# A diffusion backbone step: the held-over f tiles go, the last token slice is taken in pairs, and five pieces of code move

## The chip, the cores and the metric

One core of a Trainium2 chip runs the whole program in one launch. The metric is device time in microseconds (us). The core has TensorE (PE) for matrix products, VectorE (DVE), ScalarE (ACT), GpSimd (POOL) and SyncE (SP), which issues the DMAs. TensorE writes its sums into eight banks of 128 x 512 numbers in PSUM; DVE and ACT read them there.

## The reference

Two layers work on 640 tokens (128 context, 512 latent) of width 1024. Each layer is half an FFN, a mixer, and half an FFN; every sub-layer is wrapped in two norms with modulation.

```python
def _half_ffn(x, m, k, g_pre, g_post, w1, w2):
    h = _modulated_prenorm(x, g_pre, m, k)        # rmsnorm(x) * (1 + scale) + shift
    return x + 0.5 * m[:, 3 * k + 2, None] * _rmsnorm(_swiglu(h, w1, w2), g_post)

def _swiglu(h, w1, w2):
    gate, up = jnp.split(h @ w1, 2, axis=-1)      # 1024 -> 2 x 2816
    return (jax.nn.silu(gate) * up) @ w2          # 2816 -> 1024

for i in range(DEPTH):                            # DEPTH = 2
    xp, xs = half_ffn(xp), half_ffn(xs)           # context, latent
    # layer 0: 2-D DFT over positions and group channels between two 1024 x 1024 projections
    # layer 1: 16 heads; context attends to context, latent to an 8 x 16 neighbourhood and a cached context
    xp = xp + m_ctx[:, 5, None] * _rmsnorm(yp, norm_post[i, 1])
    xs = xs + m_lat[:, 5, None] * _rmsnorm(ys, norm_post[i, 1])
    xp, xs = half_ffn(xp), half_ffn(xs)
```

All is float32. The outputs are both token groups and the new keys and values.

## The kernel before, in words

The six sub-layers are numbered n = 0 to 5: FFN, Fourier, FFN, FFN, attention, FFN. A float32 product is made of three products of reduced type: each operand is split into `hi` (ACT, line 231) and `lo` = operand − hi (DVE, line 232), and `mm3` (lines 244 to 246) issues hi·hi, lo·hi and hi·lo. Weights come as units of 128 x 1024 (512 KB): a DMA to a `raw` tile, then the split into tiles `hi` and `lo`, of which there are six each. `unit(i)` asks for units up to three ahead of the one that is used. Activations live in a ring of 20 blocks (`ring`), split as well.

The PSUM banks have names: four `main`, two `score`, one `turn`, one `sum`.

FFN: 22 f tiles (128 of the 2816 hidden columns each). f tiles 0 to 3 are done plainly (`w1`): `multi` takes four units at a time and goes over them in turn, for half 0 (320 tokens) and then half 1. From f tile 4 on, `w1_fast` computes both halves with sums of weights and of tokens, seven blocks instead of eight, from four pieces of weights. After each slice of f tiles (`SLICES`, the last is 16 to 22), `w2` multiplies the slice's hidden rows with w2 for each of five token tiles of 128 tokens: per unit six matmuls of 512 columns into two banks; the partial sums are kept in `y` and ACT seeds the banks with them before the next slice. f tiles 20 and 21 (`LATE`) are held over: their last two products stand behind tiles 0 and 1 of the last slice (`tail`), with a weight unit made by `mix`.

When a token tile is complete, `chain` runs: ACT squares both halves (L580), the root is made (L566 on DVE, then POOL's power, L567), DVE multiplies with root and gate (L583), adds to x (L590, in the last sub-layer L628 with a DMA out), ACT sums squares (L599), DVE adds (L564), POOL takes the power again, DVE scales (L602). After a wait, counted in the planner's own estimate of TensorE's time (`yield 9000`, `tick`, `launch`), TensorE transposes the tile in eight pieces (L607) into `turn` and `sum`, ACT and DVE scale and shift them (L616, L618), and the results are split. `finish(half)` makes sure that tiles 0 to 2 (half 0) or 3 and 4 (half 1) are done before their half is used by the next sub-layer.

`gates(n)` transposes the gate columns (L548), sends them through DRAM and loads them back to all partitions as `total` (latent) and `square` (context). `gemv` (L439) is a product of the modulation on DVE with 512 KB of weights; these jobs are put in the background by `behind`.

Fourier: eight units of the input projection, half by half, `fold` on DVE (L929 to L934) after each group of four in half 1, then the two transforms and the output projection. Attention: head placements (`put`, L1057, L1076), scores (L1238), softmax (maximum by L1241, exp on ACT, L1224), context scores (L1248 to L1253), then transposes (L1274) and the output projection. The order in which instructions are put into each engine's queue comes from the order of the code, from `high_priority`, `issue_after` and `behind_of`, and from the planner's estimate; TensorE then executes its queue in that order.

## Time and profile before

| what | value |
|---|---|
| runs | 2256.93, 2260.87, 2263.44 us, median 2260.87 |
| profiled execution | 2258.16 us; its span, first to last instruction, 2256.4 us |
| busy | PE 98%, DVE 75%, ACT 52%, POOL 2% |
| mean TensorE clock | 0.996 |
| DMA | 284.20 MB, mean 126 GB/s |
| FFN 0 to Fourier | seam at about 462 us |
| Fourier to FFN 2 | seam at about 620 us |
| FFN 2 to FFN 3 | seam at about 1050 us |
| FFN 3 to attention | seam at about 1490 us |
| attention to FFN 5 | seam at about 1815 us |

Lines of the trace name an engine, a line of the kernel, the operation and its tiles as out <- in. A name in brackets is what ended the engine's idle time before the instruction.

### The profile page before, as it was taken

How to read it: one execution, taken by the hardware profiler on the slowest of the kernel's cores; microseconds unless marked ns; L12 is line 12 of the kernel's file. 1: busy time of each engine (PE TensorE's matmuls, PEld its weight loads, DVE VectorE, ACT ScalarE, POOL GpSimd, SP SyncE). 2: the span in 40 equal slices, each digit the busy share in tenths (PEclk: the TensorE clock that was granted, in tenths of full speed). 3: DMA queues.
4: the chain of work that ended last, by engine and by line, in shares of the span. 5: the costliest groups of instructions: out<-in, count | busy, mean ns of one | idle time of the engine just before them, and what ended most of it. 6: DMA issues, size and time to landing. Idle time of an engine off the chain costs nothing.

```text
span 2256.4 us, 35213 instructions
## 1 busy us (share of the span) xinstructions
PE 2210.1 (98%) x13730; PEld 2050.1 (91%) x13730; DVE 1686.8 (75%) x3079; ACT 1163.5 (52%) x2200; POOL 51.7 (2%) x95
## 2 busy tenths in 40 slices
PE   7999999999999999999999999999999999999998
PEld 5999999899799999988999999889999799999996
DVE  5898898667768898877688888675676566766674
ACT  4445454454444455446445555475778644455543
POOL 0000000000000000001000000010000000000000
PEclk9999999999999999999999999999999999999999
DMA  8144444423423344434144353523332222322223
GB/s 314 64 150 157 133 148 140 172 94 103 155 95 127 129 146 135 159 120 180 66 140 143 119 157 128 182 77 112 95 121 85 98 89 94 113 89 89 94 94 131
DMA packets 83463, 284.20 MB, mean 126 GB/s; under 512 B 9344, under 2 KB 14304, under 8 KB 83168
## 3 DMA queue, kind: packets, MB, share of 16 engines
q1 hardware_dynamic: 82752, 281.30, 37.0%
q8 instruction: 107, 1.75, 0.3%
q10 hardware_dynamic: 544, 0.66, 0.1%
q14 instruction: 60, 0.49, 0.1%
HBM read 270.34 MB, written 11.58 MB: 125 GB/s over the span
## 4 chain that ended last, share of the span: by engine, by line
PE 67%; DVE 14%; DMA 10%; ACT 5%; issue 3%; POOL 1%; SPq 0%; DVEq 0%; POOLq 0%; ACTq 0%
PE main L244 11%; PE main L246 11%; PE main L245 11%; PE score L246 5%; PE score L245 5%; PE score L244 5%; DVE lo L232 4%; DMA raw<-in_w_mod_t 3%; DMA raw<-in_w 3%; DVE junk L439 3%; PE turn L244 3%; PE turn L245 3%; PE turn L246 3%; PE sum L246 3%; PE sum L245 3%
## 5 line engine op out<-in xcount | busy, mean ns | idle before, releaser
L231 ACT ACTIVATE hi<-raw 128x1024 fp32r<-128x1024 f32 (+1 forms) x366 | 351.3, 971 | 321.0 <-PE score L245 86.1
L232 DVE TENSOR_TENSOR lo<-raw,hi 128x1024 fp32r<-128x1024 f32 (+1 forms) x366 | 406.0, 1115 | 138.8 <-ACT hi L231 137.5
L244 PE MATMUL main<-hi,ring 128*128 128x512 f32 (+2 forms) x1136 | 428.1, 379 | 2.5 <-ACT hi L231 2.5
L245 PE MATMUL main<-lo,ring 128*128 128x512 f32 (+2 forms) x1136 | 426.8, 376 | 0.9 <-DVE lo L232 0.8
L246 PE MATMUL main<-hi,ring 128*128 128x512 f32 (+1 forms) x1136 | 425.1, 375 | 1.4 <-DVE ring L232 1.4
L439 DVE SCALAR_TENSOR_TENSOR junk<-raw,wide 128x1024 bf16<-128x1024 f32 x256 | 313.2, 1224 | 102.3 <-DMA raw<-in_w_mod_t 97.6
L244 PE MATMUL score<-ring,hi 128*128 128x320 f32 x1040 | 321.8, 309 | 0.3 <-ACT left L667 0.3
L246 PE MATMUL score<-ring,lo 128*128 128x320 f32 x1040 | 321.9, 310 | 0.2 <-DVE lo L232 0.2
L245 PE MATMUL score<-ring,hi 128*128 128x320 f32 x1040 | 321.3, 309 | 0.0
L244 PEld LDWEIGHTS main<-hi,ring 128*128 128x128 f32 x1136 | 213.4, 188 | 43.1 <-ACT hi L231 4.8
L245 PEld LDWEIGHTS main<-lo,ring 128*128 128x128 f32 x1136 | 214.0, 188 | 39.7 <-DVE lo L232 3.2
L246 PEld LDWEIGHTS main<-hi,ring 128*128 128x128 f32 x1136 | 213.7, 188 | 39.3 <-DVE ring L232 1.6
L795 ACT ACTIVATE y<-main 128x512 f32<-128x512 f32 x160 | 94.2, 591 | 200.4 <-PE main L246 199.5
L244 PEld LDWEIGHTS score<-ring,hi 128*128 128x128 f32 x1040 | 195.2, 188 | 1.2 <-ACT left L667 0.6
L246 PEld LDWEIGHTS score<-ring,lo 128*128 128x128 f32 x1040 | 195.2, 188 | 1.1 <-DVE lo L232 0.6
L245 PEld LDWEIGHTS score<-ring,hi 128*128 128x128 f32 x1040 | 195.2, 188 | 0.6
L244 PE MATMUL main<-ring,hi 128*128 128x320 f32 x560 | 180.8, 323 | 1.6 <-ACT ring L231 1.6
L244 PE MATMUL turn<-ring,hi 128*128 128x320 f32 x576 | 178.9, 311 | 1.0 <-DVE left L729 0.6
L245 PE MATMUL turn<-ring,hi 128*128 128x320 f32 x576 | 178.0, 309 | 0.0
L246 PE MATMUL turn<-ring,lo 128*128 128x320 f32 x576 | 178.0, 309 | 0.0
L246 PE MATMUL main<-ring,lo 128*128 128x320 f32 x560 | 174.6, 312 | 1.8 <-DVE lo L232 1.8
L245 PE MATMUL main<-ring,hi 128*128 128x320 f32 x560 | 174.3, 311 | 1.0 <-DVE ring L232 1.0
(240 smaller groups left out, 4194.9 us busy)
## 6 DMA issues: line engine op xcount, KB each, us to landing
raw<-in_w SPq DMA_DIRECT2D x264, 512.0 KB, 3.9
raw<-in_w_mod_t SPq DMA_DIRECT2D x128, 512.0 KB, 3.5
raw<-in_qkv SPq DMA_DIRECT2D x26, 512.0 KB, 3.6
first<-in_w_mod_k SPq DMA_DIRECT2D x16, 512.0 KB, 8.7
spill<-ring SPq DMA_DIRECT2D x12, 640.0 KB, 2.9
ring<-spill SPq DMA_DIRECT2D x12, 640.0 KB, 8.5
raw<-in_bias SPq DMA_DIRECT2D x16, 448.0 KB, 3.6
raw<-in_four_in SPq DMA_DIRECT2D x8, 512.0 KB, 6.8
```

What stands on the lines that cost most here:

```text
L231: a = self.nc.scalar.activation(hi, src, AF.Copy)
L232: return a, self.nc.vector.tensor_tensor(lo, src, hi.bitcast(F32), op=ALU.subtract)
L244: mm(out, whi, xhi, start=start, stop=False)
L245: mm(out, whi, xlo, start=False, stop=False)
L246: self.latest = mm(out, wlo, xhi, start=False, stop=stop)
L439: last = self.nc.vector.scalar_tensor_tensor(out=self.junk, in0=raw, scalar=1.0, in1=self.wide[:, cond, :], op0=ALU.mult, op1=ALU.mult, ac ...
L795: nc.scalar.activation(place(i, a), bank_of(i, a), AF.Copy)
```

## The change

- The held-over f tiles go. f tiles 20 and 21 run as all others.
- In the last slice `w2` takes token tiles (0, 1), (2,), (3, 4): each unit is used for both tiles of a pair (in sub-layer 5, 3 and 4 apart). Tile 0, and tile 4 where it is in a pair, use the two `score` banks, which start empty; the sums kept in `y` are added by DVE at the head of the chain (`acc`). `out_proj` takes its tiles in the same pairs.
- `gates(n)` stands two f tiles ahead.
- In `chain`, the gate is multiplied apart from the root, and the root is multiplied and x added in one operation per piece of x. The waits before the transposes are set by tile; tiles 3 and 4 are transposed into `score` banks. The next sub-layer's first `multi` uses `turn` and `sum` instead of `score`.
- Fourier: the background jobs are spread over four places.
- Attention: one value unit is split before the placements, which stand behind its split. The context scores use one operation that adds a zero column block, stores the negated scores in SBUF and takes the minimum.

```diff
@@ chain
-    def chain(self, n, i, pss):
+    def chain(self, n, i, pss, acc=()):
...
+            for ps, a in zip(pss, acc):
+                tt(ps, ps, a, op=ALU.add)
             ss = self.col(3)
             for a, ps in enumerate(pss):
                 copy(place[:, a * WIDE : (a + 1) * WIDE], ps, AF.Square, scale=D ** -0.5, accum_out=ss[:, a : a + 1])
+            tt(pss[0], pss[0], gate[0], op=ALU.mult)
             r = self.root(ss[:, :1], ss[:, 1:2])
-            for ps, g in zip(pss, gate):
-                nc.vector.scalar_tensor_tensor(out=ps, in0=ps, scalar=r, in1=g, op0=ALU.mult, op1=ALU.mult)
+            with self.behind_of(self.rooted):
+                tt(pss[1], pss[1], gate[1], op=ALU.mult)
+            x = self.xpieces(n + 1, i)
+            for t, lo, hi in x:
+                nc.vector.scalar_tensor_tensor(out=t, in0=pss[lo // WIDE][:, lo % WIDE : lo % WIDE + hi - lo], scalar=r,
+                                               in1=t, op0=ALU.mult, op1=ALU.add)
                 if last:
-                    self.leave(n, i, pss, ps)
+                    nc.sync.dma_start(out=self.io["x_out"][i * P : (i + 1) * P, lo:hi], in_=t)
...
-            x = self.xpieces(n + 1, i)
-            for t, lo, hi in x:
-                tt(t, t, pss[lo // WIDE][:, lo % WIDE : lo % WIDE + hi - lo], op=ALU.add)
...
-        yield 9000
-        turned = [self.bank(kind) for kind in ("turn", "sum")]
+        yield {0: 10500, 1: 14000, 2: 9200, 3: 11000, 4: 15000}[i]
+        turned = [self.bank(kind) for kind in (("score", "score") if i > 2 else ("turn", "sum"))]
@@ ffn: the first multi, w2, the plan
-                                 ("main", "main", "score", "score"))
+                                 ("main", "main", "turn", "sum"))
...
+            pss = {i: seed(s, i, (s, i) in fresh) for i in tiles}
...
                 w = self.unit(base + self.w2_at[s] + f - f0)
-                x = [g[f][:, part, i * P : (i + 1) * P] for part in range(2)]
...
+                for i in tiles:
+                    x = [g[f][:, part, i * P : (i + 1) * P] for part in range(2)]
+                    new = s == 0 or (s, i) in fresh
+                    for a in range(2) if a0 is None else (a0,):
+                        cols = slice(a * WIDE, (a + 1) * WIDE)
+                        self.mm3(pss[i][a], *x, w[0][:, cols], w[1][:, cols], new and f == f0, f == f1 - 1, not new)
...
+        fresh = {(end, 0)} if final else {(end, 0), (end, 4)}
...
         for f in FAST:
+            if f == NF - 2:
+                plan += [("gates", None, None)]
             plan += [("fast", f, None)]
...
-        plan += [("mix", f, None) for f in LATE]
         plan += [("x", None, None)]
-        plan += [("w2", (due, i), None) for i in (0, 1)]
-        plan += [("tail", f, None) for f in LATE]
-        plan += [("w2", (due, i), None) for i in range(2, TILES)]
+        plan += [("w2", (due, tiles), None) for tiles in ((0, 1), (2,), (3, 4))]
@@ out_proj
-        for tiles, kind in (((0, 1), "main"), ((2,), "score"), ((3,), "main"), ((4,), "main")):
+        for tiles, kinds in (((0, 1), ("main", "main")), ((2,), ("score",)), ((3, 4), ("main", "score"))):
@@ fourier
-                kinds = ("main", "main", "main" if half or m0 else "score", "main" if half or m0 else "score")
+                kinds = ("main",) * 4 if half or m0 else ("main", "main", "turn", "sum")
...
-                    self.behind(3)
+                self.behind((2, 3, 0, 1)[2 * half + m0 // 4])
@@ attention
-        put = products([("q", 0), ("k", 0), ("q", 1), ("k", 1)], 0, ("main", "main", "score", "score"))
+        put = products([("q", 0), ("k", 0), ("q", 1), ("k", 1)], 0, ("main", "main", "turn", "sum"))
         self.finish(1)
-        with self.behind_of(*self.ready):
+        self.unit(early["v1", 0], 0)
+        with self.behind_of(*self.ready, *self.parted[early["v1", 0]]):
...
-        v_tiles(0, (0, 1), early, "score")
+        v_tiles(0, (0, 1), early)
@@ ctx_scores
-            nc.vector.tensor_reduce(out=mx, in_=ps[:, :P], axis=mybir.AxisListType.X, op=ALU.max)
-            nc.vector.tensor_scalar_mul(mx, mx, -1.0)
-            softmax(P, (c, b, p0), L, mx, ps[:, :P], 1.0)
+            nc.vector.tensor_tensor_reduce(out=L[:, :P], in0=ps[:, :P], in1=state["bm", p0][:, 512:640],
+                                           scale=-1.0, scalar=3e38, op0=ALU.add, op1=ALU.min, accum_out=mx)
+            softmax(P, (c, b, p0), L, mx, L[:, :P], -1.0)
```

In the new kernel the lines are shifted by up to 17: `mm3` is L234 to L236, the split's lo L221, the chain's adds L569, its gate multiply L573 and L576, the joined operation L579, L602 is L596, the transposes L601, `gemv` L429. The order of the two kernels shows three places.

TensorE at the start of the last slice of FFN 0, before: the first unit (`hi_3937`, `lo_3938`) is used for tile 0's two banks only, and the gates' transpose stands between them.

```order
L244 MATMUL main_1039<-hi_3937,ring_3097 128x512
L245 MATMUL main_1039<-lo_3938,ring_3097 128x512
L246 MATMUL main_1039<-hi_3937,ring_3097 128x512
L548 MATMUL turn_4037<-ident,coef 16x128
L244 MATMUL main_1040<-hi_3937,ring_3097 128x512
L245 MATMUL main_1040<-lo_3938,ring_3097 128x512
L246 MATMUL main_1040<-hi_3937,ring_3097 128x512
L244 MATMUL main_1039<-hi_3956,ring_3433 128x512
```

The same place in the new kernel:

```order
L234 MATMUL score_4113<-hi_4003,ring_3097 128x512
L235 MATMUL score_4113<-lo_4004,ring_3097 128x512
L236 MATMUL score_4113<-hi_4003,ring_3097 128x512
L234 MATMUL score_4114<-hi_4003,ring_3097 128x512
L235 MATMUL score_4114<-lo_4004,ring_3097 128x512
L236 MATMUL score_4114<-hi_4003,ring_3097 128x512
L234 MATMUL main_1039<-hi_4003,ring_3097 128x512
L235 MATMUL main_1039<-lo_4004,ring_3097 128x512
L236 MATMUL main_1039<-hi_4003,ring_3097 128x512
L234 MATMUL main_1040<-hi_4003,ring_3097 128x512
L235 MATMUL main_1040<-lo_4004,ring_3097 128x512
L236 MATMUL main_1040<-hi_4003,ring_3097 128x512
```

Tile 0 is on the two fresh `score` banks and tile 1 on `main`, and the unit serves twelve matmuls instead of six. The gates' transpose now stands among f tile 19's and 20's products.

DVE at the end of FFN 0, before: `lo_4094`, `lo_4106`, `lo_4118` and `lo_4519` are the first four weight units of the Fourier sub-layer, `ring_4031` is x of tile 3, and `main_1039` is then tile 4's bank.

```order
L232 TENSOR_TENSOR lo_4094<-raw_4091,hi_4093 128x1024
L564 TENSOR_SCALAR col_4432<-col_4430 128x1
L232 TENSOR_TENSOR ring_4238<-y,ring_4234 128x2x128
L602 TENSOR_SCALAR y<-ring_4031,col_4432 128x1024
L232 TENSOR_TENSOR lo_4106<-raw_4103,hi_4105 128x1024
L232 TENSOR_TENSOR lo_4118<-raw_4115,hi_4117 128x1024
L566 SCALAR_TENSOR_TENSOR col_4501<-col_4498 128x1
L232 TENSOR_TENSOR lo_4519<-raw_4516,hi_4518 128x1024
L583 SCALAR_TENSOR_TENSOR main_1039<-main_1039,col_4501,square_4047 128x512
```

The same place in the new kernel, where `lo_4212` and `lo_4523` are the third and fourth of those units, `main_1039` and `main_1040` are tile 3's banks and `score_4324` and `score_4325` tile 4's:

```order
L221 TENSOR_TENSOR lo_4212<-raw_4209,hi_4211 128x1024
L221 TENSOR_TENSOR lo_4523<-raw_4520,hi_4522 128x1024
L221 TENSOR_TENSOR lo_4529<-raw_4526,hi_4528 128x1024
L569 TENSOR_TENSOR score_4324<-score_4324,y 128x512
L569 TENSOR_TENSOR score_4325<-score_4325,y 128x512
L573 TENSOR_TENSOR main_1039<-main_1039,total_3835 128x512
L556 SCALAR_TENSOR_TENSOR col_4488<-col_4484 128x1
L573 TENSOR_TENSOR score_4324<-score_4324,square_3839 128x512
L576 TENSOR_TENSOR main_1040<-main_1040,total_3836 128x512
L579 SCALAR_TENSOR_TENSOR ring_4107<-main_1039,col_4488,ring_4107 128x512
L579 SCALAR_TENSOR_TENSOR ring_4107<-main_1040,col_4488,ring_4107 128x512
```

All four units are split ahead of the chains of tiles 3 and 4, which now run into one another.

DVE at the second fold of the Fourier sub-layer, before (`raw_5436` is a background job's weights):

```order
L232 TENSOR_TENSOR lo_5083<-raw_5080,hi_5082 128x1024
L439 SCALAR_TENSOR_TENSOR junk,mod<-raw_5436,wide 128x1024
L929 TENSOR_TENSOR ring_5052<-y 128x4x252
L933 TENSOR_TENSOR ring_5052<-y 128x4x63
L931 TENSOR_TENSOR y<-y 128x4x252
```

In the new kernel (`raw_5462` is then the job's weights):

```order
L221 TENSOR_TENSOR lo_5087<-raw_5084,hi_5086 128x1024
L429 SCALAR_TENSOR_TENSOR junk,mod<-raw_5462,wide 128x1024
L912 TENSOR_TENSOR ring_5066<-y 128x4x252
L916 TENSOR_TENSOR ring_5066<-y 128x4x63
L914 TENSOR_TENSOR y<-y 128x4x252
```

One product of the modulation stands ahead of the fold in both.

More of the change, by code (lines that the diff above doesn't have):

```diff
@@ L729, in w1_fast @@
                 tt(a, q, z, op=ALU.subtract)
-            if not late:
-                w = one(f, a, 2)
+            w = self.bank("sum")[:, :HALF]
+            product(f, w, 2, 0, lambda k: part(1, k), True)
+            with high():
+                tt(a, a, w, op=ALU.add)
             product(f, x, 0, 512, lambda k: self.h.chunk(4 + k, 0), False)
@@ L734, in w1_fast @@
                 nc.scalar.activation(s, x, AF.Silu)
-            product(f, z, 2, 0 if late else 512, lambda k: part(4, k), False)
+            product(f, z, 2, 512, lambda k: part(4, k), False)
             with high():
@@ L739, in w1_fast @@
                 hidden(f, v, 0)
-            if late:
-                kept[f] = a, q
-            else:
-                two(f, a, q, w, 3, 0)
-        def one(f, a, unit):
-            w = self.bank("sum" if unit is not None else "score")[:, :HALF]
-            product(f, w, unit, 0, lambda k: part(1, k), True)
-            with high():
-                tt(a, a, w, op=ALU.add)
-            return w
-        def two(f, a, q, w, unit, at):
-            product(f, w, unit, at, lambda k: self.h.chunk(4 + k, 1), False)
+            product(f, w, 3, 0, lambda k: self.h.chunk(4 + k, 1), False)
             with high():
@@ L758, in two @@
                 hidden(f, a, 1)
-        def tail(f):
-            a, q = kept[f]
-            two(f, a, q, one(f, a, None), None, 512)
-        banks, seeded = [], set()
+        banks, ready = [], {}
         place = lambda i, a: self.wide_y[:, i * D + a * WIDE : i * D + (a + 1) * WIDE]
-        bank_of = lambda i, a: banks[(2 * i + a) % 4]
-        def seed(s, i):
-            if s and (s, i) not in seeded:
-                seeded.add((s, i))
-                with self.tc.high_priority():
-                    for a in range(2):
-                        nc.scalar.activation(bank_of(i, a), place(i, a), AF.Copy)
@@ L775, in w2, with seed @@
-        def w2(s, i):
+        def seed(s, i, fresh=False):
+            if (s, i) in ready:
+                return ready[s, i]
             if not banks:
                 banks.extend(self.bank() for _ in range(4))
-            f0, f1 = SLICES[s]
-            seed(s, i)
-            if i and i + 1 < TILES:
-                seed(s, i + 1)
-            elif i == 0:
-                seed(s, 1)
-            ends = n == self.subs - 1 and s == len(SLICES) - 1 and i == TILES - 1
+            if fresh:
+                ready[s, i] = [self.bank("score") for _ in range(2)]
+                return ready[s, i]
+            at = 2 * turn.index(i) % 4
+            pss = ready[s, i] = banks[at : at + 2]
+            if s:
+                with self.tc.high_priority():
+                    for a, ps in enumerate(pss):
+                        nc.scalar.activation(ps, place(i, a), AF.Copy)
+            return pss
@@ L786, in w2 @@
+        def w2(s, tiles):
+            f0, f1 = SLICES[s]
+            ends = n == self.subs - 1 and s == len(SLICES) - 1 and tiles[-1] == TILES - 1
+            pss = {i: seed(s, i, (s, i) in fresh) for i in tiles}
+            after = turn[turn.index(tiles[-1]) + 1 :] if tiles[-1] in turn else []
+            for i in after[:1]:
+                seed(s, i)
             for a0, f in [(a, f) for a in range(2) for f in range(f0, f1)] if ends else [(None, f) for f in range(f0, f1)]:
                 w = self.unit(base + self.w2_at[s] + f - f0)
-                x = [g[f][:, part, i * P : (i + 1) * P] for part in range(2)]
@@ L799, in ffn @@
+            for i in tiles:
+                ps = ready.pop((s, i))
+                if f1 == NF:
+                    boundary(i, ps, [place(i, a) for a in range(2)] if (s, i) in fresh else ())
+                else:
+                    with self.tc.high_priority():
+                        for a in range(2):
+                            nc.scalar.activation(place(i, a), ps[a], AF.Copy)
         passed = done = 0
+        end = len(SLICES) - 1
+        final = n == self.subs - 1
+        fresh = {(end, 0)} if final else {(end, 0), (end, 4)}
@@ L800, in ffn @@
+        turn = list(range(TILES))
         for op, a, half in self.ffn_plan:
+            if op == "w2" and a[0] == end:
+                turn = [i for i in range(TILES) if (end, i) not in fresh]
             if op == "w1":
@@ L852, in plan_ffn @@
                 self.ffn_units += [("gate", v, 0), ("sums", v, 1)]
[L853 removed]
+                self.ffn_units += [(kind, None, None) for kind in ("up", "all")]
             elif op == "w1":
```

68 lines of the change are left out of this document (20 added, 48 removed).

## The prediction

> **What bounds the kernel now.** I read the engine totals first, then two windows beside each other, then the list of what TensorE waited for, and last single stretches of the timeline.
>
> ```profile
> span 2256.4 us, 35213 instructions
> PE 2210.1 (98%) x13730; PEld 2050.1 (91%) x13730; DVE 1686.8 (75%) x3079; ACT 1163.5 (52%) x2200; POOL 51.7 (2%) x95
> ...
> 445.00:486.00 41.00, 39.59 (x220) 34.49 (x220) 33.72 (x75) 31.13 (x74) 5.58 (x7) 1.00 0.23 76
> 486.00:516.00 30.00, 30.00 (x207) 30.00 (x206) 13.62 (x28) 5.32 (x11) 0.00 (x0) 1.00 0.31 105
> 537.50:541.20 3.70, 3.62 (x18) 3.62 (x19) 3.61 (x8) 0.90 (x3) 0.00 (x0) 0.55 0.19 33
> 1007.00:1014.00 7.00, 5.38 (x21) 3.35 (x19) 4.93 (x5) 4.42 (x6) 0.00 (x0) 1.00 0.57 206
> ```
>
> TensorE is the bound (98%). A window row gives its limits and width, then busy time of PE, PEld, DVE, ACT and POOL, the granted clock, the DMA share and GB/s. Inside a stage (486 to 516) TensorE never stops: 207 matmuls in 30 us, 0.145 us each for the 320-column form. At a seam between two stages (445 to 486, the end of FFN 0) it has holes, while DVE and ACT are at 82% and 76%. The number of matmuls is the same after the change, so only holes can go.
>
> ```profile
> PE turn L607 <- DVE y L602: 6.3, 11, 1.2
> PE main L244 <- ACT hi L231: 2.5, 3, 0.9
> PE score L1238 <- ACT left L1224: 2.1, 3, 0.9
> PE main L246 <- DVE lo L232: 1.8, 3, 0.6
> ...
> PE main L246 <- DVE ring L232: 1.4, 1, 1.4
> PE score L245 <- DVE lo L232: 1.3, 1, 1.3
> PE score L1238 <- DVE col L1241: 1.3, 2, 0.9
> PE sum L607 <- DVE y L618: 1.3, 2, 0.7
> ...
> PE main L245 <- DVE lo L232: 0.8, 1, 0.8
> ...
> PE turn L244 <- DVE left L729: 0.6, 2, 0.4
> PE score L244 <- DVE left L749: 0.6, 1, 0.6
> ...
> PE turn L548 <- DVE right L737: 0.5, 1, 0.5
> ```
>
> Each row: who waited for what, total us, times, longest. These rows understate a hole, since ends of matmuls are modelled. The start of the last slice in FFN 2 shows by how much:
>
> ```profile
> 1007.62 0.39 PE L245 MATMUL main<-lo,ring 128*128 128x512 f32 x1
> 1007.85 0.39 PE L246 MATMUL main<-hi,ring 128*128 128x512 f32 x1
> 1009.09 0.50 PE L244 MATMUL main<-hi,ring 128*128 128x512 f32 x1 [0.86 <-ACT hi L231]
> 1010.35 0.50 PE L245 MATMUL main<-lo,ring 128*128 128x512 f32 x1 [0.76 <-DVE lo L232]
> ```
>
> Starts lie 0.23 us apart when nothing waits. The two steps of 1.24 and 1.26 us cost 1.01 and 1.03, where the rows say 0.86 and 0.76. So I add 0.2 us per wait (0.15 and 0.27).
>
> **The change, part by part.**
>
> *Transposes (L607), 6.3 + 1.3 us in 13 waits, with 0.2 each 10.2 us.* A tile's transposes are put 9 us behind its last matmul, and its y is later than that:
>
> ```profile
> 470.94 0.58 ACT L580 ACTIVATE y<-main 128x512 f32<-128x512 f32 x1
> 473.25 1.22 DVE L232 TENSOR_TENSOR lo<-raw,hi 128x1024 fp32r<-128x1024 f32 x1
> 473.49 1.38 POOL L567 TENSOR_TENSOR col<-col,power 128x1 f32<-128x1 f32 x1 [3.28 <-DVE col L566]
> 477.78 0.67 DVE L590 TENSOR_TENSOR ring<-ring,main 128x512 f32<-128x512 f32 x1
> 481.62 0.75 DVE L602 TENSOR_SCALAR y<-ring,col 128x1024 f32<-128x1024 f32 x1 [0.44 <-POOL col L567]
> 483.76 1.36 DVE L618 TENSOR_SCALAR y<-sum,coef 128x128 f32<-128x128 f32 x4
> ```
>
> Tile 4 of FFN 0 needs from 470.94 to 482.37, 11.4 us, of which foreign splits (L232) and the slow root (1.38 us) are some 4. The change puts transposes 9.2 to 15 us behind, by tile, and takes about 1.2 us off the chain (below). By the order, the worst place is behind FFN 0: after the last pair 75 matmuls stand ahead of tile 3's transposes (75 x 0.145 = 10.9 us) and 106 and those eight transposes ahead of tile 4's (about 16.3 us). DVE's work up to tile 4's y is: two adds into the fresh banks and four gate multiplies at 0.67 (4.0), four joined operations at about 0.7 (2.8), three splits at 1.22 (3.7), three products of the modulation at 1.22 (3.7), two L602 at 0.75 (1.5), and tile 3's L618 and splits (1.36 and about 1.4); with small ones 18 us, some 1.5 late. Elsewhere no product of the modulation stands there and I get 11 to 13 us against 14 to 16, in time. So 2.0 us of the 10.2 stay where two tiles end together; **−8.2**, and +1.1 of new wait at FFN 0 (the 1.5 less what overlaps the wait of tile 3).
>
> *The pair in the last slice.* A weight unit feeds six matmuls per tile, 1.38 us; its split takes 1.22 on DVE alone, beside the chains. For tiles 0 and 1 together it feeds 2.76. The four waits of the last slice's first tile (hi L231 2.5 in 3, lo L245 0.8 in 1; 3.3 + 0.8) go: **−4.1**. The bank seeds that go from ACT come back as two DVE adds per fresh tile (1.35 us, beside matmuls). The two late f tiles run as the others; their additional splits (half a unit each) and DMA queue places lie beside 24 matmuls of 0.145 per unit, 3.5 us against 1.22. Cost nothing; the cover is the clean stretch 486 to 516, where DVE is 45% busy. Without it they would cost 0.6 us per f tile at most.
>
> *Start of the next stage.* The first four units' lo splits stand, in the order, ahead of the last pair's chains where before they stood between them. The three waits main L246 <- lo (1.8 + 0.6) go: **−2.4**.
>
> *Late f tiles and gates.* Waits of the held-over products and of the gates' transposes (L729 in part, L749, L548; 1.7 us in 4, 2.5 with the allowance) go with the early gates; some may come back in the new f tiles: **−2.0**.
>
> *Context scores.* One DVE operation into SBUF takes the place of a maximum and a sign change:
>
> ```profile
> L1224 ACT ACTIVATE left<-score,col x16: 350/367/368, 1568.8 to 1763.0; 128x128 f32<-128x128 f32 x16
> L1251 DVE TENSOR_REDUCE col<-score x16: 272/291/294, 1566.9 to 1761.2; 128x1 f32<-128x128 f32 x16
> L1252 DVE TENSOR_SCALAR col<-col x16: 132/154/155, 1567.3 to 1761.5; 128x1 f32<-128x1 f32 x16
> L1241 DVE CUSTOM_DVE_ANT_0 left<-score,raw x48: 536/557/559, 1549.0 to 1756.8; 128x384 f32<-128x384 f32 x48
> ```
>
> The bank is then free at the end of DVE's operation and not, up to 0.9 us later, when ACT's 0.367 is done. The three waits on L1224 (2.1 + 0.6) go: **−2.7**. The two on L1241 stay. The new operation is not in this trace; its bounds are L1251 alone (0.29) and the like operation of L1241, which has three times the columns (0.56), so per call −0.16 to +0.11 us against 0.45 now, −2.6 to +1.8 us for all 16 if all of it showed. It is nearer to the first, and DVE has waits of its own here; I take 0.
>
> *Attention entry.* A value unit is split ahead of the head placements and no longer behind them. Of the wait score L245 <- lo (1.3 + 0.2) I take **−1.0**, and +0.5 for the placements that are now behind.
>
> *Fourier.* The modulation's products are spread, but by the order one still stands ahead of the second fold, and it waits for its weights:
>
> ```profile
> 532.79 1.23 DVE L439 SCALAR_TENSOR_TENSOR junk<-raw,wide 128x1024 bf16<-128x1024 f32 x1 [0.96 <-DMA raw<-in_w_mod_t]
> 537.58 0.39 PE L246 MATMUL main<-hi,ring 128*128 128x258 f32 x1 [1.38 <-DVE ring L232]
> ```
>
> So the wait of 1.4 us stays, and what follows it: the first 3.70 us behind it ran at a clock of 0.55 (the third window above), 1.7 us lost. I take 0; bounds are −3.1 (wait and slow clock go) and +1.4 (another such product ahead). [...]
>
> *Tail.* The last tile's path runs in the open:
>
> ```profile
> 2248.44 0.39 PE L246 MATMUL main<-hi,ring 128*128 128x512 f32 x1
> 2249.22 0.60 ACT L580 ACTIVATE y<-main 128x512 f32<-128x512 f32 x1 [3.68 <-PE main L246]
> 2249.94 0.16 DVE L566 SCALAR_TENSOR_TENSOR col<-col 128x1 f32<-128x1 f32 x1 [4.97 <-ACT y L580]
> 2250.25 0.54 POOL L567 TENSOR_TENSOR col<-col,power 128x1 f32<-128x1 f32 x1 [7.91 <-DVE col L566]
> 2250.82 1.42 DVE L583 SCALAR_TENSOR_TENSOR main<-main,col,square 128x512 f32<-128x512 f32 x2 [0.72 <-POOL col L567]
> 2252.14 1.28 DVE L628 TENSOR_TENSOR ring<-ring,main 128x512 f32<-128x512 f32 x2
> ```
>
> After the root come two passes now (2250.82 to 2253.42, 2.60 us), and one after the change (1.42): **−1.2**. The gate multiply (0.67) runs beside the root (0.54) and ends with it. If it held POOL up as the split at 473.25 did (1.38 instead of 0.54), 0.4 would be left.
>
> The sum: −8.2 −4.1 −2.4 −2.0 −2.7 −1.0 −1.2 = −21.6, new waits +1.6, together −20.0 us. The profiled execution took 2258.16 (span 2256.4 and 1.8 around it), so **2238 us**. It lies 0.1% below the median of the runs, 2260.87; 0.3% of that (2254.1 and 2267.7) is about what a measurement can tell from no change.
>
> **The rivals.**
>
> *A, half of the seams' gain is eaten.* Tiles 3 and 4 now end together and their chains share DVE and ACT, and so do tiles 0 and 1. For it: DVE was 82% busy at the seam with the tiles apart. Against: the launches are up to 6 us later. Two late transposes of 1 us at each of five seams are +10: 2248.
>
> *B, slower.* Tile 3's chain used to start six units (8.2 us) ahead of tile 4's end, and lay under matmuls; now both chains must end within half 0 of the next stage, eight units x 24 x 0.145 = 27.8 us, or half 1 waits for them. One chain takes 470.94 to about 486 (15 us); two in a row with foreign splits between may take 25 to 30. It decides from 33 us on: 5.4 us at each of five seams are +27, less the 20 gained, 2265; a little more is slower. Against it: they overlap on different engines, and the sum above gives 18 us to tile 4's y, about 22 to its end.
>
> *C, no change.* Each seam's wait only hands over to what is late next (splits for chains), and 5 us of other places are left: 2253 to 2256. Against: the rows name several causes at places far apart (the attention, the tail), which do not depend on each other.
>
> **How the numbers follow.** My forecast 60%, A 22%, C 11%, B 5%, and 2% for less than 2230. Low: without the new waits (−1.6) and the 2.0 left, and with the Fourier wait and its slow clock gone (−3.1), 2231; I take 2230. High: A's 2248 with +1.8 of the context operation, 2250, and C's lower end takes a little of the chance: I take 2252. Between these lie most of the forecast and of A, eight in ten. Faster than 2254.1: the forecast, A, the 2% and a small part of C, 0.85; the same 0.11; slower 0.04.
>
> **What would show it.** In the profile after, the row turn L607 <- y should shrink from 11 waits to 3 or 4, and rows for hi and lo on main at the last slice's start should be gone; score <- L1224 should be gone; L439's wait ahead of the fold and a window clock near 0.55 should still be there; from the last matmul to the span's end 6.8 us instead of 8.0. I am wrong if score transposes (tiles 3, 4) wait more than 1.5 us each at most seams (A), if the first product of half 1 waits for splits of y (B), or if weights' splits are late in the middle of a stage, where nothing waits now.

## The result, and the profile after

| | before | changed |
|---|---|---|
| median, us | 2259.43 (2256.93 to 2263.44, 4 runs) | 2237.9 (2233.9 to 2238.73, 4 runs) |
| ratio | | 0.990, 95% interval 0.988 to 0.9919 |
| profiled execution: span, us | 2256.4 | 2236.9 |

The forecast was 2238. The total is right, but the seams gained 6.6 us more than was booked and the scores lost 5.9 us more, and the two cancel. First the totals of the profile of the changed kernel, then its list of what TensorE waited for (total us, times, longest), which answers to the list of before:

```profile
span 2236.9 us, 35214 instructions
PE 2202.2 (98%) x13730; PEld 2053.1 (92%) x13730; DVE 1690.2 (76%) x3093; ACT 1156.5 (52%) x2186; POOL 43.8 (2%) x95
...
PE main L1258 <- ACT left L1242: 3.7, 4, 1.9
...
PE main L236 <- DVE ring L221: 2.8, 1, 2.8
...
PE score L1222 <- DVE col L1225: 1.4, 2, 1.0
PE main L234 <- DVE ring L1059: 1.0, 1, 1.0
...
PE main L235 <- DVE lo L221: 0.9, 1, 0.9
...
PE score L601 <- DVE y L596: 0.7, 1, 0.7
```

Of the 13 waits of the tiles' transposes (7.6 us; 11 for y, two for the bank that the tile before was in) one is left, 0.7 us; the weights' waits at the last slice are gone, and so are those of the scores for the exp. New are 3.7 us, instead of 0.5, in which the transposes of the scores wait for ACT's scaling (L1242, which was L1258), and the wait in the Fourier sub-layer is 2.8 instead of 1.4 us. At the ends of FFN 0, FFN 2 and FFN 3 TensorE is now as busy as inside a stage. Windows of the changed kernel (limits, width, busy PE, PEld, DVE, ACT, POOL, clock, DMA share, GB/s) there:

```profile
434.00:485.00 51.00, 51.00 (x280) 45.25 (x279) 41.32 (x87) 33.21 (x82) 6.20 (x10) 1.00 0.31 103
995.00:1050.00 55.00, 55.00 (x285) 47.75 (x284) 36.65 (x72) 29.99 (x66) 3.21 (x6) 1.00 0.44 160
1438.00:1500.00 62.00, 62.00 (x340) 54.73 (x338) 44.46 (x97) 34.97 (x88) 5.34 (x10) 1.00 0.38 137
```

The kernel can be cut at marks that both versions have: the first and last matmul of the full w2 slices, the first and last latent score matmul, the last matmul, the end. Stretches in us, from the starts of these matmuls in the profiled execution of each kernel (e1 to e12 are the experiments below):

| kernel | FFN 0, to the end of slice 3 | seam to FFN 2's first w2 | seam FFN 2 to 3 | seam FFN 3 to first score | scores | last score to FFN 5's first w2 | FFN 5 slice 3 to last matmul | tail |
|---|---|---|---|---|---|---|---|---|
| before | 362.1 | 329.4 | 182.3 | 159.3 | 209.0 | 131.6 | 104.8 | 7.9 |
| changed | 363.3 | 323.1 | 175.9 | 154.4 | 212.1 | 128.8 | 102.5 | 6.4 |
| e1 old context scores | 362.3 | 319.7 | 175.9 | 154.4 | 208.5 | 129.6 | 102.5 | 6.4 |
| e2 tile of ones | 361.5 | 323.9 | 176.2 | 154.4 | 208.3 | 129.5 | 102.5 | 6.4 |
| e3 before, new scores | 362.9 | 329.0 | 183.9 | 160.0 | 211.1 | 130.7 | 104.7 | 7.6 |
| e4 pinned | 364.6 | 319.0 | 175.9 | 154.4 | 211.9 | 128.7 | 102.5 | 6.4 |
| e5 launches at 9 us | 364.4 | 324.2 | 177.3 | 156.1 | 211.0 | 129.4 | 102.5 | 6.4 |
| e6 single tiles | 362.4 | 319.5 | 176.4 | 154.8 | 211.1 | 128.7 | 102.5 | 6.4 |
| e7 no join | 362.8 | 321.3 | 179.2 | 157.7 | 211.1 | 129.3 | 102.5 | 7.6 |
| e8 both mends | 360.9 | 318.5 | 175.9 | 154.4 | 208.3 | 129.5 | 102.5 | 6.4 |
| e9 before, no held-over f | 364.7 | 327.3 | 179.9 | 157.8 | 208.9 | 131.6 | 102.6 | 7.6 |
| e10 before, new launches | 363.1 | 321.7 | 181.2 | 161.2 | 208.5 | 129.4 | 104.5 | 7.6 |
| e11 gates late | 362.7 | 322.9 | 176.1 | 154.4 | 212.8 | 128.7 | 102.6 | 6.4 |
| e12 e8, old entry | 360.4 | 318.7 | 175.9 | 157.9 | 208.4 | 129.5 | 102.5 | 6.4 |

The full slices in FFN 2, 3 and 5, left out here, take 256.5 to 257.6 each. The first column varies by 4 us between executions of equal code, and the second holds the Fourier wait, which varies too (below). The scores with the changed kernel's operand lie between 211.0 and 212.8, all others between 208.3 and 209.0; the other columns repeat to some tenths where the code is the same. From before to changed the seams and FFN 5's last slice give −22.7 us, the scores +3.2, the tail −1.6, the rest +1.7: −19.4 of a span that is 19.5 shorter.

### The profile page after: what moved, and what is told of

Its sections match the earlier page's. It is cut to its first block, busy times and chain, and to the rows that moved or that the text cites. A ratio compares the mean times of both kernels' runs of the same rounds, so it can differ in the third digit from the quotient of the medians.

```text
span 2236.9 us, 35214 instructions
## 1 busy us (share of the span) xinstructions
PE 2202.2 (98%) x13730; PEld 2053.1 (92%) x13730; DVE 1690.2 (76%) x3093; ACT 1156.5 (52%) x2186; POOL 43.8 (2%) x95
## 4 chain that ended last, share of the span: by engine, by line
PE 79%; DVE 11%; DMA 5%; issue 2%; ACT 2%; POOL 0%; SPq 0%; DVEq 0%; POOLq 0%; ACTq 0%
PE main L234 12%; PE main L236 11%; PE main L235 11%; PE score L234 6%; PE score L236 6%; PE score L235 6%; PE turn L234 4%; PE turn L235 4%; PE turn L236 4%; PE sum L234 4%; PE sum L235 4%; PE sum L236 4%; DMA raw<-in_w_mod_t 3%; DVE junk L429 3%; DVE lo L221 3%
## 5 line engine op out<-in xcount | busy, mean ns | idle before, releaser
L221 DVE TENSOR_TENSOR lo<-raw,hi 128x1024 fp32r<-128x1024 f32 (+1 forms) x374 | 415.5, 1117 | 134.6 <-ACT hi L220 133.2
L234 PE MATMUL main<-hi,ring 128*128 128x512 f32 (+2 forms) x1044 | 391.4, 375 | 0.0
L236 PE MATMUL main<-hi,ring 128*128 128x512 f32 (+2 forms) x1044 | 387.7, 372 | 2.8 <-DVE ring L221 2.8
L429 DVE SCALAR_TENSOR_TENSOR junk<-raw,wide 128x1024 bf16<-128x1024 f32 x256 | 312.9, 1222 | 101.6 <-DMA raw<-in_w_mod_t 96.7
L235 PE MATMUL main<-lo,ring 128*128 128x512 f32 (+2 forms) x1044 | 388.0, 372 | 0.9 <-DVE lo L221 0.9
L236 PE MATMUL score<-ring,lo 128*128 128x320 f32 x896 | 277.1, 309 | 0.3 <-DVE lo L221 0.2
L234 PE MATMUL score<-ring,hi 128*128 128x320 f32 x896 | 277.3, 309 | 0.0
L235 PE MATMUL score<-ring,hi 128*128 128x320 f32 x896 | 276.8, 309 | 0.0
L236 PEld LDWEIGHTS main<-hi,ring 128*128 128x128 f32 x1044 | 196.3, 189 | 37.3 <-DVE ring L221 3.1
L234 PEld LDWEIGHTS main<-hi,ring 128*128 128x128 f32 x1044 | 196.7, 188 | 34.6 <-issue 1.4
L235 PEld LDWEIGHTS main<-lo,ring 128*128 128x128 f32 x1044 | 196.7, 188 | 33.8 <-DVE lo L221 1.1
L234 PE MATMUL turn<-ring,hi 128*128 128x320 f32 x648 | 200.6, 310 | 0.7 <-DVE left L714 0.7
L234 PE MATMUL sum<-ring,hi 128*128 128x320 f32 x648 | 200.3, 309 | 0.0
L236 PE MATMUL sum<-ring,lo 128*128 128x320 f32 x648 | 200.2, 309 | 0.0
L235 PE MATMUL turn<-ring,hi 128*128 128x320 f32 x648 | 200.2, 309 | 0.0
L236 PE MATMUL turn<-ring,lo 128*128 128x320 f32 x648 | 200.2, 309 | 0.0
L235 PE MATMUL sum<-ring,hi 128*128 128x320 f32 x648 | 200.2, 309 | 0.0
L234 PE MATMUL main<-ring,hi 128*128 128x320 f32 x560 | 181.2, 324 | 2.6 <-ACT ring L220 1.6
L235 PE MATMUL main<-ring,hi 128*128 128x320 f32 x560 | 174.7, 312 | 1.1 <-DVE ring L221 1.0
L236 PE MATMUL main<-ring,lo 128*128 128x320 f32 x560 | 174.6, 312 | 0.0
```

The source lines that it names most:

```text
L221: self.last_split = a, self.nc.vector.tensor_tensor(lo, src, hi.bitcast(F32), op=ALU.subtract)
L234: mm(out, whi, xhi, start=start, stop=False)
L235: mm(out, whi, xlo, start=False, stop=False)
L236: self.latest = mm(out, wlo, xhi, start=False, stop=stop)
L429: last = self.nc.vector.scalar_tensor_tensor(out=self.junk, in0=raw, scalar=1.0, in1=self.wide[:, cond, :], op0=ALU.mult, op1=ALU.mult, ac ...
```

## The experiments

The kernel before, timed beside them, had a median of 2258.2 us with e1 to e4, 2262.3 with e5 to e8 and 2259.7 with e9 to e12. So a difference of a median to the changed kernel's 2237.9 is uncertain by some 3 us; where ratios to the kernel before say something else, both are given, and the stretches above decide.

### The scores that became slower: e1, e2, e3

e1 goes back to the old context scores, e2 keeps the new operation with another operand, e3 puts the new one alone into the kernel before (the reverse of e1's edit).

```diff
 e1
-            nc.vector.tensor_tensor_reduce(out=L[:, :P], in0=ps[:, :P], in1=state["bm", p0][:, 512:640], ...
-            softmax(P, (c, b, p0), L, mx, L[:, :P], -1.0)
+            nc.vector.tensor_reduce(out=mx, in_=ps[:, :P], axis=mybir.AxisListType.X, op=ALU.max)
+            nc.vector.tensor_scalar_mul(mx, mx, -1.0)
+            softmax(P, (c, b, p0), L, mx, ps[:, :P], 1.0)
 e2
-            nc.vector.tensor_tensor_reduce(out=L[:, :P], in0=ps[:, :P], in1=state["bm", p0][:, 512:640], ...
+            nc.vector.tensor_tensor_reduce(out=L[:, :P], in0=ps[:, :P], in1=self.ones[:, :P], ...
```

> The changed kernel with the context scores as before (maximum, sign change, exp from PSUM); all else as changed. From the first latent score matmul to the first matmul of the output projection the kernel before took 222.5 us, the changed one 225.7. Theory H: the zero columns belong to the bias tile, which is so held one block longer; it sits in one of four raw tiles, so the modulation's weights come later and their 1.22 us products are put among the softmaxes. Then this stretch is back at about 222.5 us, the waits main <- ACT left (scale of the exp) fall from 3.7 us to under 1, waits of score <- exp are back with about 2 us, and the time is 2233.5 to 2236. Rival R1: the new operation does gain its 2.7 us and something else of the change lengthens the stretch: 228 us, total 2240.5. Rival R2: the new operation is itself slow where it stands: also 222.5, but then e2 does not gain.

> The changed kernel, but the context scores add a constant tile of ones that is always in SBUF (a constant does not change a softmax) instead of the zero columns of the bias tile: same operation, same bank, bias tile not held. H: the modulation's products stand where they did before, the exp no longer holds the bank: 222.5 - 2.7 = about 220 us for the stretch, total 2231.5 to 2233.5. R1: 225.7, total 2238. R2: 225.7, total 2238.

> The kernel before with only the new context scores (zero columns of the bias tile). H: the stretch grows from 222.5 to 225 to 226 us, total about 3 us above the kernel before. R1, and the recorded prediction: 2.7 us less, 220. R2: as H, which e2 tells apart.

Measured: e1 2235.22 (2230.49 to 2238.21), e2 2233.55 (2231.13 to 2235.3), e3 2261.13 with a ratio of 1.001 (1.000 to 1.002) to the kernel before. The stretch of the scores decides better than the medians: 212.1 falls to 208.5 (e1) and 208.3 (e2), and rises from 209.0 to 211.1 in e3. (The expectations count up to the output projection, a stretch that is longer by a constant part.) H is right and R1 and R2 are out: not the operation but its operand costs 2 to 4 us. (In e11's 212.8 TensorE's clock may have a part: its mean is 0.995 in that execution and 0.997 in the changed kernel's.) The hold shows in SyncE's queue, where the weights of the modulation are issued, and the first score matmul; before, then changed, then e2:

```profile
1546.64 0.86 PE L1238 MATMUL score<-ring,ring 128*128 128x384 f32 x4
1648.53 0.33 SPq L173 DMA_DIRECT2D raw<-in_w_mod_t  x1
```

```profile
1530.67 0.86 PE L1222 MATMUL score<-ring,ring 128*128 128x384 f32 x4
1638.90 0.34 SPq L172 DMA_DIRECT2D raw<-in_w_mod_t  x1
```

```profile
1529.58 0.86 PE L1222 MATMUL score<-ring,ring 128*128 128x384 f32 x4
1629.83 0.33 SPq L172 DMA_DIRECT2D raw<-in_w_mod_t  x1
```

From the first score the DMA is issued after 101.9 us, 108.2 us and 100.3 us. What then happens in the changed kernel, DVE first, then TensorE:

```profile
1708.37 1.22 DVE L429 SCALAR_TENSOR_TENSOR junk<-raw,wide 128x1024 bf16<-128x1024 f32 x1
...
1710.94 1.22 DVE L221 TENSOR_TENSOR lo<-raw,hi 128x1024 fp32r<-128x1024 f32 x1
1712.24 1.33 DVE L1059 TENSOR_TENSOR ring<-main,ring 64x128 fp32r<-64x128 f32 x4
1713.58 0.16 DVE L1209 RECIPROCAL col<-col 128x1 f32<-128x1 f32 x1
...
1714.73 0.55 PE L1258 MATMUL main<-ident,left 128*128 128x128 f32 x3 [1.89 <-ACT left L1242]
```

DVE is full from 1708 on (busy 3.97 of the 4.00 us to 1712); the reciprocal (L1209) that ACT's scaling needs comes behind a late product, a split and four head placements, and TensorE waits 1.89 us. In e2 the row main <- left L1242 is 0.5 us in all. The gain that was forecast, and that e2's expectation still counted on (220 us by its count, where 222 came), however, is not there either: e2, whose scores no longer wait for the exp, takes 208.3 us and e1, where three such waits (1.5 us) are back, 208.5.

### The Fourier wait and its clock: e4

```diff
     def gemv(self, raw, layer, j, conds=(0, 1)):
         for cond in conds:
-            last = self.nc.vector.scalar_tensor_tensor(...)
+            with self.behind_of(*self.folded):
+                last = self.nc.vector.scalar_tensor_tensor(...)
...
+        self.folded = (last_fold,)
         self.out_proj(0, base + NCH + 2, boundary)
```

`last_fold` is the second fold's last operation; `folded` is emptied after the first of the output projection's products.

> The changed kernel, but the modulation's products that belong behind the second fold of the Fourier sub-layer are held behind it in DVE's queue. Theory F: the fold, whose inputs are there at about 530 us, is held up at 532.7 by a product that waits for its weights (2.44 us). Then TensorE's wait of 2.9 us falls under 1, the clock of 0.54 in the 3.7 us behind it is 1.00 (1.7 us), and the time is 2233 to 2235. Rival F1: products that come later keep their raw tiles longer, the output projection's weights come late, and the wait goes there: 2237 to 2239. Rival F2 (the clock falls for another reason than this wait): the wait goes and 0.54 stays, 2235 to 2236.

Measured: 2232.68 (2231.49 to 2235.61), 5.2 us under the changed kernel. Windows of the changed kernel at this place, then of e4 at the same:

```profile
533.20:536.30 3.10, 0.31 (x4) 0.06 (x3) 3.10 (x6) 0.00 (x0) 0.00 (x0) 1.00 0.01 5
536.30:540.00 3.70, 3.64 (x18) 3.65 (x19) 3.42 (x6) 0.90 (x3) 0.00 (x0) 0.54 0.22 49
```

```profile
530.00:533.50 3.50, 3.50 (x30) 2.90 (x31) 3.42 (x4) 3.30 (x11) 0.00 (x0) 1.00 0.40 144
533.50:537.20 3.70, 3.70 (x31) 3.07 (x32) 3.70 (x6) 1.04 (x5) 0.00 (x0) 1.00 0.03 10
```

The wait is gone and the clock stays at 1.00: 323.1 to 319.0 in the second column. F is right, F1 and F2 are out. The slow clock came with the wait and went with it; e8, which has the same pin, has neither (clock 1.00 from 525 to 545 us), and e12, which has it too, has no row of this wait.

### Launches, pairs and the joined operation: e5, e6, e7

```diff
 e5
-        yield {0: 10500, 1: 14000, 2: 9200, 3: 11000, 4: 15000}[i]
+        yield 9000
 e6
-        plan += [("w2", (due, tiles), None) for tiles in ((0, 1), (2,), (3, 4))]
+        plan += [("w2", (due, (i,)), None) for i in range(TILES)]
...
-        fresh = {(end, 0)} if final else {(end, 0), (end, 4)}
+        fresh = set()
 e7
-            tt(pss[0], pss[0], gate[0], op=ALU.mult)
             r = self.root(ss[:, :1], ss[:, 1:2])
-            with self.behind_of(self.rooted):
-                tt(pss[1], pss[1], gate[1], op=ALU.mult)
+            for ps, g in zip(pss, gate):
+                nc.vector.scalar_tensor_tensor(out=ps, in0=ps, scalar=r, in1=g, op0=ALU.mult, op1=ALU.mult)
...
-                nc.vector.scalar_tensor_tensor(out=t, in0=pss[...], scalar=r, in1=t, op0=ALU.mult, op1=ALU.add)
+                tt(t, t, pss[...], op=ALU.add)
```

> The changed kernel with the transposes put 9 us behind a tile's last matmul, as before; all else as changed. The recorded working: y is ready 10.5 us after the last pair for tile 3 and 11 to 18 us for tile 4, and 13 to 14 us for tile 1; at 9 us TensorE waits 1 to 2 us for the first tile of a pair and 2 to 6 for the second, at five seams: +20 to +35 us, 2258 to 2273, slower than or equal to the kernel before. Rival: the shorter chain does most of it and the later launch only the rest, at most 1 us per tile of a pair: 2243 to 2248.

> The changed kernel with the last slice's tiles one by one on seeded banks (no pairs, no fresh banks, no adds at the chain's head); launch times as changed. The recorded working: the last slice's first tile waits for weight units again (4.1 us in four waits in the kernel before) and the next stage's first units are split late again (2.4 us): +6.5, 2244.5. Rival P: the early gates and the f tiles without held-over products already leave time for these splits: 2238 to 2240.

> The changed kernel with root and gate in one operation and x added in a second one, as before. The recorded working: from the last matmul to the end 1.2 us longer (6.3 now, 8.0 before, so up to 1.6), each chain's y 1.2 us later, which shows at the end of FFN 0 where y is already late (two tiles, 1.2 to 2.4 us) and where tiles 0 and 1 end together: total +2.5 to +4, 2240.5 to 2242. Rival: the chains have room everywhere and only the tail shows: +1.2 to 1.6, 2239.3.

e5: 2243.84 (2242.89 to 2244.96), +5.9, or +5.0 by the ratios (0.9922 against 0.990): the rival was right, and the sum worked out from the prediction's ready times was far too high. In e5's list of waits y (L596) is late twice, by at most 0.3 us; seven more waits of the transposes, 2.4 us in all, are for the banks that the tile before still holds (L610, L612). So the later launches mostly keep two tiles' transposes apart here.

e6: 2234.42 (2233.6 to 2235.35), 3.5 us under the changed kernel. The pair is not needed for the weights: none of the four waits at the last slice is back. Rival P is right. The gain lies in the second column, where e6 had little of the Fourier wait (0.5 us) and no slow clock (1.00 from 525 to 545 us); whether single tiles bring that about by their timing or the executions fell so is not settled. At the two seams without that, pairs are worth 0.5 us each (176.4 against 175.9, 154.8 against 154.4), where a unit's split comes 0.4 us late at the next stage's start.

e7: 2244.37 (2241.95 to 2244.78), +6.5, or +5.0 by the ratios (0.9922), more than both expectations. The tail is 1.26 us longer, as expected; two seams are 3.3 us longer each, and a wait is there that no other version with pairs has. From e7's timeline, ACT then TensorE, and last ACT at the same place of the changed kernel:

```profile
450.16 0.60 ACT L749 ACTIVATE main<-y 128x512 f32<-128x512 f32 x1 [3.59 <-DVE ring L578]
```

```profile
450.81 0.50 PE L234 MATMUL main<-hi,ring 128*128 128x512 f32 x1 [1.09 <-ACT main L749]
```

```profile
447.97 1.26 ACT L751 ACTIVATE main<-y 128x512 f32<-128x512 f32 x2 [2.34 <-DVE ring L579]
```

ACT seeds tile 3's banks (L749, L751) when tile 1's chain has read them for the last time. With the joined operation that is at 447.97, without it at 450.16, and TensorE stands for it, three times 1.1 to 1.5 us. The join shortens the time for which a bank is held, and not only the way to y. It is probably worth more than the median says: in e7's profiled execution DVE's order at the Fourier fold differs and the Fourier wait is gone, as in e4, to which e7 loses 8.4 us (2242.2 against 2233.8 us of span).

### The kernel before with one part each: e9, e10; gates late: e11

```diff
 e9 (before)
-LATE = (NF - 2, NF - 1)
+LATE = ()
 e10 (before)
-        yield 9000
+        yield {0: 10500, 1: 14000, 2: 9200, 3: 11000, 4: 15000}[i]
 e11 (changed)
-            if f == NF - 2:
-                plan += [("gates", None, None)]
...
-        plan += [("x", None, None)]
+        plan += [("x", None, None), ("gates", None, None)]
```

> The kernel before with no held-over f tiles (20 and 21 run as all others; single token tiles, launches at 9 us, late gates, all else as before). Theory L, after e6: the last slice's first units are late in the kernel before because each held-over f tile keeps one of four raw tiles until its mixed unit is made, so the DMA of the next unit is issued late (the hi of 1007.99 waits 3.41 us for its DMA). Then the waits main <- hi L231 and lo L232 at the last slice's start (1008, 1448, 2204) go here without any pair: -4 us; and the seven us of products that no longer stand behind tile 1 make tile 0's and 1's transposes no later. Total 2254 to 2256 against 2259.4. Rival G: the early gates took them away; then they stay here, 2258 to 2260. Rival P: the lost cover costs more transposes' waits than the units gain: 2260 to 2263.

> The kernel before with only the launch times of the transposes as changed (10.5, 14, 9.2, 11 and 15 us by tile instead of 9). The recorded working: up to 8.2 us of waits for y go: 2251 to 2253. e5 says that in the changed kernel the launch times are worth 5.9 us. Rival: later launches push the splits of the transposed tiles into those of the next stage's units and the gain is half of that: 2255 to 2257.

> The changed kernel with the gates' transposes ahead of the last slice, as before, instead of two f tiles earlier. Theory L: units of the last slice are on time all the same; the gates come 14 us later, and the first chain is 16 us behind the last slice's start now, while the gates took some 10 us to come back: the same as the changed kernel within 1 us, 2237 to 2239. Rival G: the waits at the last slice's start come back (4 us, L548 included) : 2241 to 2243.

e9: 2251.88, ratio 0.9967 (0.9957 to 0.9977), 7.8 us less: theory L, with more than its range. The rows main <- hi and main <- lo of the last slice are gone. The row of the kernel before that I should have read in the first place, ACT at the start of FFN 2's last slice:

```profile
1007.99 1.06 ACT L231 ACTIVATE hi<-raw 128x1024 fp32r<-128x1024 f32 x1 [3.41 <-DMA raw<-in_w]
```

The split is late because its weights are; ACT had been idle for 3.41 us. Here are two DMAs for weights from the kernel before's chain of work that ended last, with their start and us; the second is this unit's:

```profile
994.05 3.52 DMA raw<-in_w
1001.47 6.43 DMA raw<-in_w
```

It was issued when a split had freed a raw tile (DVE's lo, which ended at 1001.45), and then took 6.43 us. At the other two places, FFN 3 and FFN 5, the weights had landed before ACT took them (in FFN 3 at 1447.72), and ACT was splitting a held-over tile's mixed unit (`ring<-raw`) ahead of them (in FFN 5 from 2203.07, the unit itself from 2204.02); in FFN 3:

```profile
1447.53 1.04 ACT L231 ACTIVATE ring<-raw 128x1024 fp32r<-128x1024 f32 x1
1448.48 1.04 ACT L231 ACTIVATE hi<-raw 128x1024 fp32r<-128x1024 f32 x1
```

e9 also has a new wait, the one of e7, since tile 0's banks are wanted 7 us sooner by tile 2 and the old chain is long:

```profile
PE main L244 <- ACT main L773: 3.0, 3, 1.0
```

e10: 2251.52, ratio 0.9967 (0.9954 to 0.998), 8.2 us less, as recorded. (At the attention's entry it loses 1.9 us to a new wait and a slow clock behind it, 0.66 from 1513 to 1517 us, and gains the more elsewhere. In the profiled execution of e9 the Fourier clock stayed at 1.00, as the last section shows, where the kernel before lost 1.7 us; that does not belong to the edit. The mean clock is 0.997 in e10's and 0.996 in the kernel before's.) e11: 2236.46 (2232.65 to 2238.08): the early gates are worth nothing, theory L.

### Both mends, and the attention's entry: e8, e12

```diff
 e12 (e8 with)
-        self.unit(early["v1", 0], 0)
-        with self.behind_of(*self.ready, *self.parted[early["v1", 0]]):
+        with self.behind_of(*self.ready):
```

> The changed kernel with both mends: the constant tile of ones (e2: 2233.55) and the pinned products (e4: 2232.68), which lie 80 % of the kernel apart. If they add up, 2237.9 - 4.35 - 5.2 = 2228.3. If they share a cause, 2232.

> e8 (ones and pinned products, 2229.23) with the attention entry's value unit as before, not split ahead of the placements. The changed kernel waits 1.0 + 1.2 us there (lo, and a placement), the kernel before 1.6 (lo). If the entry's reorder is what costs, 0.6 us less than e8: 2228.6; if it gains what was recorded (1.0 - 0.5), 2229.7. Neither can be told by the time alone; the seam from FFN 3's last full slice to the first score matmul (154.35 in e8, 159.25 before) tells.

e8: 2229.23 (2227.7 to 2231.25), ratio 0.9858 (0.9843 to 0.9873) to the kernel before: the mends add up (2228.3 expected), and it beats both kernels. e12: 2232.35, above both of its expectations, and the seam is 157.9 instead of 154.4: beside e8 the reordered entry is worth 3.5 us in the profiled executions and 3.1 by the medians, not 0.5. Without it TensorE waits twice, here e12's timeline, because the value unit's hi stands behind the placements in ACT's queue:

```profile
1497.20 0.69 PE L235 MATMUL main<-hi,ring 128*128 128x256 f32 x2 [1.97 <-ACT hi L221]
1498.74 0.58 PE L236 MATMUL main<-lo,ring 128*128 128x256 f32 x1 [0.84 <-DVE lo L222]
```

Waits are the smaller part of it. e8 waits here too, 0.85 and 0.98 us by its rows, so the waits differ by 1.0 us (1.1 by the starts). The other 2.4 us go with the clock, which is 0.50 for 6.83 us behind e12's waits; in the changed kernel, which has the same waits and the same 154.4 us as e8, it is 1.00 from 1497 to 1512 us. From e12:

```profile
1497.35:1504.18 6.83, 5.99 (x27) 5.69 (x28) 4.20 (x8) 3.54 (x6) 1.79 (x3) 0.50 0.41 144
```

## Why the prediction was right, point by point

- *Transposes, −8.2, with a new wait of 1.1 at FFN 0.* Right, and better than booked: 2.0 us of the old waits were to stay, and none did. The launch times alone give 8.2 us in the kernel before (e10), with two waits for y left (1.6 us); that this is the booked number to a tenth is luck, since e10 has losses and gains elsewhere too. At FFN 0 the last pair's matmul starts at 468.64 and tile 4's y is done at 485.98, 17.3 us behind, where 18 were worked out; TensorE waits there, 0.68 us by its row (0.84 by the starts), and at no other seam:

```profile
468.64 0.39 PE L236 MATMUL score<-hi,ring 128*128 128x512 f32 x1
...
486.13 0.63 PE L601 MATMUL score<-ident,y 128*128 128x128 f32 x4 [0.68 <-DVE y L596]
...
485.24 0.74 DVE L596 TENSOR_SCALAR y<-ring,col 128x1024 f32<-128x1024 f32 x1
```

- *The pair, −4.1.* The waits went, by another part. The step that failed is "a weight unit feeds six matmuls per tile, 1.38 us; its split takes 1.22": the rate of splitting was not the limit, the held-over tiles were. e9 removes the waits without a pair and e6 keeps them away. How they did it differs by place: in FFN 2 the unit's DMA came late, in FFN 3 and FFN 5 the mixed unit's split stood ahead on ACT (both above). By the code each held-over tile also keeps one of four raw tiles until its mixed unit is made; that this hold delayed the DMA in FFN 2 fits e9, which took the whole holding over away, but is not shown by itself, nor is the reason of the transfer's 6.43 us.
- *Start of the next stage, −2.4.* The waits are gone. In e6 half of each is back (0.4 of 0.8 us at three seams), so half of this is the pair's.
- *Late f tiles and gates, −2.0.* The gates give nothing (e11). The held-over tiles alone are worth 7.8 us (e9) against the −4.1 − 2.0 that was booked for them and for the pair.
- *Context scores, −2.7.* Wrong in sign: +3.2 us for the stretch. The step costed the operation, and that takes what was said:

```profile
L1235 DVE CUSTOM_DVE_ANT_0 left<-score,raw x16: 272/291/293, 1551.0 to 1748.5; 128x128 f32<-128x128 f32 x16
```

  (the changed kernel's 16 calls; 0.291 us, as L1251 before). It did not ask what its operand keeps from being reused. With that mended (e2 against e1) the gain is 0.1 us: what is late next took its place, rival C's way at this one place.
- *Attention entry, −1.0 and +0.5.* Mis-sized. Against the kernel before the waits got no shorter: the one for lo (1.3 us) went, and the changed kernel has two, 0.9 us for lo and 1.0 us for a placement (L235 <- lo and L234 <- ring L1059 in its list), so −1.3 and +1.9. Against the other parts of the change without this one, it is worth 3.5 us (e12), of which 2.4 are the clock; the forecast had no term for that.
- *Fourier, 0, bounds −3.1 and +1.4.* The wait grew by 1.5 us in the profiled execution, with the slow clock as before (0.54 behind it, 0.55 in the kernel before). Left out was that this wait differs between executions, since the product ahead of the fold waits for its weights (0.1 to 2.8 us by its rows). With the same order of DVE's instructions around the fold it was 2.9 us in the changed kernel, 3.3 in e2, 2.0 in e5, 1.8 in e11, 1.3 in e1 and 0.6 in e6 (by the starts).
- *Tail, −1.2.* Right: 7.94 to 6.38; of these 1.56 us the join is 1.26 (7.64 in e7), and the gate multiply did not hold POOL up. From the changed kernel's last rows:

```profile
2231.84 0.69 DVE L576 TENSOR_TENSOR main<-main,square 128x512 f32<-128x512 f32 x1
2232.07 0.54 POOL L557 TENSOR_TENSOR col<-col,power 128x1 f32<-128x1 f32 x1 [7.62 <-DVE col L556]
2232.64 1.41 DVE L579 SCALAR_TENSOR_TENSOR ring<-main,col,ring 128x512 f32<-128x512 f32 x2
```

- *The join elsewhere* was booked only as 1.2 us less to each y. It is worth 5 to 6.5 us by e7's median, and some 8 by its profiled execution beside e4's; 1.26 of that is the tail, and the rest shows where banks come free sooner.
- *The sum.* For the seams (transposes, pair, stage start, f tiles, entry and the new waits) −16.1 had been booked and −22.7 came; for the scores −2.7 and +3.2; for the tail −1.2 and −1.6. Two errors of 6 us cancel. That the total came out right is luck in that measure; the forecast of a gain at the seams is not.
- *Rivals.* A did not come: but for the 0.7 us at FFN 0, y is ready in time behind the shared chains, and even with launches at 9 us it is late only twice, by at most 0.3 us (e5). B's half 1 never waited for a split of y. C came at one place.

## What to carry to other kernels

An operand has two prices: the time to read it and the time for which its buffer is kept from the next user. The second was 2 to 4 us here for sixteen operations that were themselves no slower, and it showed far away, in other DMAs and in the order of another engine. The same holds for PSUM banks: an operation that reads a bank for the last time 2 us sooner (447.97 against 450.16 in e7) was worth more at the bank than on its own path. When a row says that a split is late, read the engine's own row first: if that engine was idle and waiting for a DMA, or busy with another unit that could be left out, more time per unit is not the cure.
